# Eight of ten row norms: spread over the partitions through DRAM in place of products with the identity

## The chip, the cores and the metric

The kernel runs on one core of one Trainium2 chip. The metric is the time of one execution on the device in microseconds (us); three executions of the kernel before are shown, and their median is the time before. A profile is one execution taken by the hardware profiler. The engines are named as in the profile: PE is TensorE, DVE is VectorE, ACT is ScalarE, POOL is GpSimd and SP is SyncE, which here issues transfers.

## The reference, cut to what matters

Two blocks run one after the other over x of 512 tokens and 1024 features, in float32. The first has two hybrid layers (retention, pooling, neighbourhood attention and attention to a memory, side by side behind gates), each with a feed-forward part; the second has an "even" layer (sliding window and latent attention) and an "odd" one (dilated attention), each followed by cross attention to a memory and a feed-forward part.

```python
def rms_norm(x, g):
    xf = x.astype(jnp.float32)
    y = xf * lax.rsqrt(jnp.mean(xf * xf, axis=-1, keepdims=True) + EPS)
    return (y * g.astype(jnp.float32)).astype(x.dtype)
...
def hybrid_layer(x, mem, norm_mix_g, ...):
    h = rms_norm(x, norm_mix_g)
    proj = h @ w_in
...
    x = x + merged @ w_out
    a, g = jnp.split(rms_norm(x, norm_ffn_g) @ w_ffn_in, 2, axis=-1)
    return x + (jax.nn.silu(a) * g) @ w_ffn_out
...
    for layer in range(DEPTH):
        x = x + mixers[layer](rms_norm_2(x, mix_norms[layer]))
        x = x + memory_cross_attention(rms_norm_2(x, xn), rms_norm_2(mem, mn), wq, wkv, wo)
        x = x + swiglu(rms_norm_2(x, fn), wg, wu, wd)
    return rms_norm_2(x, final_norm)
```

So x is normalised ten times before a product (two hybrid layers, even, odd, two cross attentions, four feed-forward parts), and once at the end. Inside even, two more norms stand over the latent vectors cq and ckv.

## The kernel before, in words

x lies feature-major: eight tiles X of 128 features by 512 tokens. Next to it lies H, x times the gain, split into a high and a low part in float32r. A weight matrix is streamed in chunks of 512 KB: a transfer on SP's queue brings it into `ws` (two buffers), ACT casts it to the high part `wh` (L265, three buffers), DVE takes the difference `wl` (L266), and every product is three matmuls, high by high, low by high and high by low (L273 to L275, or L317 to L319 in the hybrid, even and odd layers where columns are 256 wide). A chunk feeds 24 matmuls. The results go to PSUM banks with the names p_acc, p_S and p_O; p_T is the bank of transposes and of the norms.

The product does not wait for the norm of x: it is made of x times the gain, and each result is multiplied afterwards, as it leaves PSUM, by 1/rms of its token. While x is updated, `prep` adds its squares into `acc`. `stats` then makes the norm: four small matmuls with a column of ones give the sum of each token, tokens on the partitions (a 128x4 tile); a Newton iteration on DVE (L340 to L347) makes `rtok_x` of it. To multiply a feature-major result, 1/rms must stand in a row over all tokens, the same on all 128 partitions: the tile `R_x`, 128x512. `spread` makes it: four fp32 matmuls of rtok, one column at a time broadcast to 128x128, with the identity (L368), into one p_T bank, and a copy by ACT (L371):

```python
        for i in range(4):
            nc.tensor.matmul(out=pb[:, 128 * i:128 * i + 128], lhsT=r[:, i:i + 1].to_broadcast([128, 128]),
                             rhs=self.ident, start=True, stop=True)
        R = self.tabp.tile([128, 512], F32, name="R_" + name, tag="R", bufs=3)
        nc.scalar.copy(R, pb)
```

Where R_x is used first: in a feed-forward part (`ffn`), DVE multiplies the first result of the gate by it (`fa`, L700). In the hybrid, even and odd layers it is multiplied into the rope tables (`ropeC`, L730, or `rope`), and `rope` (L480 to L491) empties the PSUM bank: four copies by ACT to `ru` (L484, L485), DVE's `ru` (L486) and `rc` (L488), which is the last to read the bank, and the sum (L491). In even, `norm_stats` is called twice more, for cq and ckv (`rtok_cq`, `rtok_ckv`, `R_cq`, `R_ckv`), a few instructions at a time beside sliding-window attention: scores (L476, L477) in p_S, DVE's and ACT's softmax into P (L519), transposes (L554) and their copy PT, and products with the values into p_O. The transposes of the memory (L664) and its products (`mh`, `ml`) follow there. The first hybrid layer weaves the neighbourhood attention in the same way between weight products (scores L476/L477, softmax L501 to L511, transposes L554, PT L561, values L928).

The order of the instructions on each engine is set by the scheduler of the language, which plays the program through a timeline of its own and puts weights 200 places ahead (AHEAD); the code's order is only its input. All transfers go by SP's queue. Among them the two that matter for comparison: `rpd<-rpb_p` writes 120 pieces of 192 bytes to DRAM (L1408), and `x<-xd` reads 256 KB.

Of the kernel before, what the change touches and what calls it, by code (L numbers as in the profile page):

```python
# [9 lines left out]
F32 = mybir.dt.float32  # L10
# [7 lines left out]
D = 1024  # L18
# [70 lines left out]
def run(gen):  # L89
    for _ in gen:  # L90
        pass


def weave(main, fill, rate, lead=0.0):

    due = lead
    for _ in main:
        due += rate
        while due >= 1.0:
            due -= 1.0  # L100
            next(fill, None)
# [29 lines left out]
def pipeline(pairs):  # L131

    prev = None
    for p, pair in enumerate(pairs):
        if p == 0 and pair.prep:
            pair.prep()
            yield
        for i in range(pair.n):
            state = pair.first(i)
            yield  # L140
            if prev:
                prev[0].second(*prev[1:])
                if prev[1] == prev[0].n - 1:
                    prev[0].done()
                yield
            prev = (pair, i, state)
            if i == 2 and p + 1 < len(pairs) and pairs[p + 1].prep:
                pairs[p + 1].prep()
    prev[0].second(*prev[1:])
    prev[0].done()  # L150
    yield


class Net:
# [196 lines left out]
                g.tensor_tensor(out=y, in0=y, in1=t, op=OP.mult)  # L351
        return y

    def norm_stats(self, acc, dim, name, want_bc=True):

        nc = self.nc
        ps = self.psum("T")
        for i in range(4):
            nc.tensor.matmul(out=ps[:, i:i + 1], lhsT=acc[:, 128 * i:128 * i + 128], rhs=self.ones, start=True, stop=True)
        r = self.rsqrt(ps[:, 0:4], 4, 1.0 / dim, self.sm.tile([128, 4], F32, name="rtok_" + name, tag="rtok", bufs=4), fast=True)  # L360
        return r, self.spread(r, name) if want_bc is True else None

    def spread(self, r, name):

        nc = self.nc
        pb = self.psum("T")
        for i in range(4):
            nc.tensor.matmul(out=pb[:, 128 * i:128 * i + 128], lhsT=r[:, i:i + 1].to_broadcast([128, 128]),  # L368
                             rhs=self.ident, start=True, stop=True)
        R = self.tabp.tile([128, 512], F32, name="R_" + name, tag="R", bufs=3)  # L370
        nc.scalar.copy(R, pb)  # L371
        return R

    def prep(self, k, g, start=False):
# [13 lines left out]
            gf = self.vec("final_norm_2", 8)  # L388
            nc.vector.tensor_scalar(out=self.X[k], in0=self.X[k], scalar1=gf[:, k:k + 1], scalar2=None, op0=OP.mult)

    def stats(self, want_bc=True):
        return self.norm_stats(self.acc, D, "x", want_bc)

    def head_stats(self, sq, nt, r):

# [957 lines left out]
    def cross(self, l, kv, g_next):  # L1353
        nc, a = self.nc, self.a
        p = f"l{l}_"
        mk, mv = kv()
        _, R = self.stats()
        heads = [None] * 4
        q = [self.at(name="xq") for _ in range(4)]

        def pair(h):
            st = {}
            c, b = h // 2, h % 2

            def first(i):
                if i == 0:
                    st["O"] = self.psum("O")
                Ps = []
                for t in range(2 * i, 2 * i + 2):
                    Sp = self.psum("S")[:, :256]  # L1370
                    nc.tensor.matmul(out=Sp, lhsT=q[h][:, 128 * t:128 * t + 128], rhs=mk[c][:, b, :], start=True, stop=True)
                    Ps.append(self.softmax(Sp, 256, X_SCALE))
                return Ps

            def second(i, Ps):
                pt = self.transposes([Ps[t][:, 128 * j:128 * j + 128] for j in range(2) for t in range(2)])
                for j in range(2):
                    nc.tensor.matmul(out=st["O"][:, 256 * i:256 * i + 256], lhsT=mv[c][:, j, 128 * b:128 * b + 128],
                                     rhs=pt[:, 256 * j:256 * j + 256], start=j == 0, stop=j == 1)

            def done():
                heads[h] = self.split(st["O"])
            return Pair(first, second, done, n=2)

        def project(c, tags):
            return self.proj_steps(self.H, a[p + "w_xq_2"], 256 * c, 256,
                                   lambda j, ps: nc.vector.tensor_tensor(out=q[2 * c + j], in0=ps, in1=R, op=OP.mult), tags=tags)

        Wo = a[p + "w_xo_2"]
        run(project(0, WIDE))  # L1390
        fill = project(1, ("acc",))
        weave(pipeline([pair(0), pair(1)]), fill, 0.5)
        run(fill)
        fill = self.residual_steps(heads[:2], Wo, 0, 2, 1.0, False, ("acc",), 0, 4)
        weave(pipeline([pair(2), pair(3)]), fill, 0.5)
        run(fill)
        self.residual(heads[2:], Wo, 2, 2, 1.0, g_next, WIDE, 0, 4)
        self.residual(heads, Wo, 0, 4, 1.0, g_next, WIDE, 4, 8)
# [121 lines left out]
```

## Time and profile before

| | |
|---|---|
| median of 3 executions | 3081.18 us (3078.11 to 3083.54) |
| profiled execution, its own time | 3081.58 us |
| its span in the profile | 3079.8 us |
| PE busy | 3011.1 us (98%) |
| DVE busy | 1706.3 us (55%) |
| ACT busy | 1248.5 us (41%) |
| POOL busy | 312.4 us (10%) |
| packets of the transfers | 288594, 285.61 MB, mean 93 GB/s |

The span runs from the first to the last instruction in the profile; the execution's own time holds a little more. Busy time is a share of the whole span. Matmuls overlap their neighbours, so the time that one holds the path is read from the chain or from the distance of two starts, not from its duration.

### The profile page before, as it was taken

The page shows a single profiled execution, that of the slowest core. Times are in us where ns is not written, and L with a number is a line of the kernel's source. Part 1 is how long each engine was busy: PE and PEld are TensorE (multiplying, and loading weights), DVE is VectorE, ACT ScalarE, POOL GpSimd, SP SyncE. Part 2 cuts the span into 40 slices and gives each one's busy share as a digit, 9 for nine tenths or more (in the row PEclk, how much of TensorE's full clock was granted, in tenths as well). Part 3 has the DMA queues.
Part 4 walks back from the last instruction along what each step waited for, and adds up shares of the span by engine and source line. Part 5 has one row for each costly group of instructions (what it writes and reads, how often), then busy time and mean ns, then how long its engine had stood idle before and what let it go on. Part 6 is the DMA issues. An engine that isn't in the chain of part 4 may idle for free.

```text
span 3079.8 us, 39014 instructions
## 1 busy us (share of the span) xinstructions
PE 3011.1 (98%) x15087; PEld 2479.5 (81%) x15087; DVE 1706.3 (55%) x2984; ACT 1248.5 (41%) x2102; POOL 312.4 (10%) x491
## 2 busy tenths in 40 slices
PE   7999999999999999999999899999999999999998
PEld 6777888888888878888888777788888777888887
DVE  7466465444565755654446676654446766464444
ACT  5445233222453533432224654432225766442222
POOL 4210120010132012010010000010010000010100
PEclk9999999999999999999999999999999999999999
DMA  5322243333332223333323222233333211233332
GB/s 170 104 64 71 92 127 96 96 97 99 126 116 87 82 83 109 119 95 98 96 89 96 78 61 62 72 96 96 96 89 96 69 56 62 89 103 96 96 96 82
DMA packets 288594, 285.61 MB, mean 93 GB/s; under 512 B 23700, under 2 KB 280089, under 8 KB 288409
## 3 DMA queue, kind: packets, MB, share of 16 engines
q1 hardware_dynamic: 288409, 283.13, 30.3%
q8 instruction: 118, 1.93, 0.3%
q14 instruction: 67, 0.55, 0.1%
HBM read 275.37 MB, written 7.71 MB: 92 GB/s over the span
## 4 chain that ended last, share of the span: by engine, by line
PE 90%; DVE 5%; DMA 1%; issue 1%; ACT 1%; POOL 1%; SPq 0%; DVEq 0%; ACTq 0%; POOLq 0%
PE p_acc L273 11%; PE p_acc L274 11%; PE p_acc L275 11%; PE p_S L273 7%; PE p_S L274 7%; PE p_S L275 7%; PE p_O L274 7%; PE p_O L275 7%; PE p_O L273 7%; PE p_acc L317 2%; PE p_acc L318 2%; PE p_acc L319 2%; PE p_T L554 2%; PE p_O L858 1%; DVE wl L266 1%
## 5 line engine op out<-in xcount | busy, mean ns | idle before, releaser
L266 DVE TENSOR_TENSOR wl<-ws,wh 128x1024 fp32r<-128x1024 f32 (+1 forms) x516 | 618.8, 1200 | 738.6 <-ACT wh L265 737.4
L265 ACT CAST wh<-ws 128x1024 fp32r<-128x1024 f32 (+1 forms) x516 | 516.7, 1002 | 1095.7 <-issue 352.9
L273 PE MATMUL p_acc<-hh,wh 128*128 128x512 f32 x1064 | 418.7, 394 | 4.4 <-DVE rs_t L344 1.7
L274 PE MATMUL p_acc<-hh,wl 128*128 128x512 f32 x1064 | 416.6, 392 | 0.0
L275 PE MATMUL p_acc<-hl,wh 128*128 128x512 f32 x1064 | 415.0, 391 | 0.0
L704 POOL TENSOR_TENSOR fa<-fa,R_x 128x512 f32<-128x512 f32 x88 | 115.2, 1310 | 1524.9 <-DVE fa L703 1524.9
L274 PE MATMUL p_O<-hh,wl 128*128 128x512 f32 x656 | 255.5, 390 | 0.0
L275 PE MATMUL p_O<-hl,wh 128*128 128x512 f32 x656 | 255.5, 389 | 0.0
L273 PE MATMUL p_O<-hh,wh 128*128 128x512 f32 x656 | 254.7, 389 | 0.0
L274 PE MATMUL p_S<-hh,wl 128*128 128x512 f32 x640 | 249.6, 391 | 2.7 <-DVE wl L266 2.7
L273 PE MATMUL p_S<-hh,wh 128*128 128x512 f32 x640 | 249.6, 392 | 2.4 <-ACT wh L265 2.4
L275 PE MATMUL p_S<-hl,wh 128*128 128x512 f32 x640 | 249.6, 391 | 0.0
L273 PEld LDWEIGHTS p_acc<-hh,wh 128*128 128x128 f32 x1064 | 199.7, 188 | 49.3 <-issue 3.6
L275 PEld LDWEIGHTS p_acc<-hl,wh 128*128 128x128 f32 x1064 | 199.7, 188 | 41.6 <-issue 0.8
L274 PEld LDWEIGHTS p_acc<-hh,wl 128*128 128x128 f32 x1064 | 199.9, 188 | 40.3 <-issue 1.7
L273 PE MATMUL p_acc<-ah,wh 128*128 128x512 f32 x468 | 185.0, 397 | 1.4 <-ACT ah L243 1.4
L274 PE MATMUL p_acc<-ah,wl 128*128 128x512 f32 x468 | 182.5, 390 | 0.0
L275 PE MATMUL p_acc<-al,wh 128*128 128x512 f32 x468 | 182.4, 393 | 0.0
L274 PEld LDWEIGHTS p_S<-hh,wl 128*128 128x128 f32 x640 | 120.8, 189 | 28.4 <-DVE wl L266 3.4
L274 PEld LDWEIGHTS p_O<-hh,wl 128*128 128x128 f32 x656 | 123.1, 188 | 25.5
L273 PEld LDWEIGHTS p_O<-hh,wh 128*128 128x128 f32 x656 | 123.1, 188 | 25.5
L275 PEld LDWEIGHTS p_O<-hl,wh 128*128 128x128 f32 x656 | 123.2, 188 | 25.3
(385 smaller groups left out, 5623.7 us busy)
## 6 DMA issues: line engine op xcount, KB each, us to landing
ws<-w_ffn_in SPq DMA_DIRECT2D x88, 512.0 KB, 3.6
ws<-w_gate SPq DMA_DIRECT2D x64, 512.0 KB, 3.7
ws<-l_w_gate SPq DMA_DIRECT2D x44, 512.0 KB, 4.0
ws<-l_w_up SPq DMA_DIRECT2D x44, 512.0 KB, 3.7
ws<-w_ffn_out SPq DMA_DIRECT2D x40, 512.0 KB, 3.5
ws<-l_w_down SPq DMA_DIRECT2D x40, 512.0 KB, 3.5
ws<-w_in SPq DMA_DIRECT2D x36, 512.0 KB, 3.8
ws<-l_w_qkv SPq DMA_DIRECT2D x24, 512.0 KB, 3.5
```

The costliest lines, as they stand in the source:

```text
L265: nc.scalar.copy(wh, st)
L266: nc.vector.tensor_tensor(out=wl, in0=st, in1=wh.bitcast(F32), op=OP.subtract)
L273: nc.tensor.matmul(out=out, lhsT=wh[part, k, cols], rhs=hh[part, hn], start=start, stop=False)
L274: nc.tensor.matmul(out=out, lhsT=wl[part, k, cols], rhs=hh[part, hn], start=False, stop=False)
L275: nc.tensor.matmul(out=out, lhsT=wh[part, k, cols], rhs=hl[part, hn], start=False, stop=stop)
L317: nc.tensor.matmul(out=o, lhsT=hh[:, t0:t0 + 128], rhs=wh[:, kk, :], start=k == 0, stop=False)
L318: nc.tensor.matmul(out=o, lhsT=hh[:, t0:t0 + 128], rhs=wl[:, kk, :], start=False, stop=False)
L319: nc.tensor.matmul(out=o, lhsT=hl[:, t0:t0 + 128], rhs=wh[:, kk, :], start=False, stop=k == K - 1)
L554: nc.tensor.transpose(pt[:, 128 * i:128 * i + 128], b, self.ident)
L704: nc.gpsimd.tensor_tensor(out=a, in0=a, in1=R, op=OP.mult)
L858: nc.tensor.matmul(out=O[64 * b:64 * b + 64, :], lhsT=rv[i // 2][:, i % 2, 64 * h:64 * h + 64], rhs=Ps[b], start=i == 0, stop=i == 3)
```

## The change

For eight of the ten norms of x, `stats` now calls `spread_far` in place of `spread`: a first transfer writes the 128x4 tile of rtok to a row of 512 numbers in DRAM (element by element, since token i*128+p lies on partition p), and a second reads that row into all 128 partitions of R. Both are issued on ACT's queue; the second waits there for the first to land. The two cross attentions (`near=True`) and cq and ckv keep `spread`. Each of the eight has a row of its own in DRAM.

```diff
--- before.py
+++ after.py
@@ -351,14 +351,14 @@
                 g.tensor_tensor(out=y, in0=y, in1=t, op=OP.mult)
         return y
 
-    def norm_stats(self, acc, dim, name, want_bc=True):
+    def norm_stats(self, acc, dim, name, want_bc=True, near=True):
 
         nc = self.nc
         ps = self.psum("T")
         for i in range(4):
             nc.tensor.matmul(out=ps[:, i:i + 1], lhsT=acc[:, 128 * i:128 * i + 128], rhs=self.ones, start=True, stop=True)
         r = self.rsqrt(ps[:, 0:4], 4, 1.0 / dim, self.sm.tile([128, 4], F32, name="rtok_" + name, tag="rtok", bufs=4), fast=True)
-        return r, self.spread(r, name) if want_bc is True else None
+        return r, (self.spread if near else self.spread_far)(r, name) if want_bc is True else None
 
     def spread(self, r, name):
 
@@ -369,6 +369,16 @@
                              rhs=self.ident, start=True, stop=True)
         R = self.tabp.tile([128, 512], F32, name="R_" + name, tag="R", bufs=3)
         nc.scalar.copy(R, pb)
+        return R
+
+    def spread_far(self, r, name):
+
+        nc = self.nc
+        self.spreads = getattr(self, "spreads", 0) + 1
+        row = self.dr.tile([1, 512], F32, name=f"row{self.spreads}", tag=f"row{self.spreads}")
+        R = self.tabp.tile([128, 512], F32, name="R_" + name, tag="R", bufs=3)
+        nc.scalar.dma_start(out=row.rearrange("o (i p) -> p (o i)", p=128), in_=r)
+        nc.scalar.dma_start(out=R, in_=row.to_broadcast([128, 512]))
         return R
 
     def prep(self, k, g, start=False):
@@ -388,8 +398,8 @@
             gf = self.vec("final_norm_2", 8)
             nc.vector.tensor_scalar(out=self.X[k], in0=self.X[k], scalar1=gf[:, k:k + 1], scalar2=None, op0=OP.mult)
 
-    def stats(self, want_bc=True):
-        return self.norm_stats(self.acc, D, "x", want_bc)
+    def stats(self, want_bc=True, near=False):
+        return self.norm_stats(self.acc, D, "x", want_bc, near)
 
     def head_stats(self, sq, nt, r):
 
@@ -1354,7 +1364,7 @@
         nc, a = self.nc, self.a
         p = f"l{l}_"
         mk, mv = kv()
-        _, R = self.stats()
+        _, R = self.stats(near=True)
         heads = [None] * 4
         q = [self.at(name="xq") for _ in range(4)]
 
```

In the new file the lines behind L373 stand ten lower (L554 is L564 there, L476 is L486). What the scheduler makes of it is shown at three places.

ACT in the first feed-forward part, around the copy of R_x (ft is the tanh of the gate, ah the high part of the hidden vector). Before:

```order
286 L246 ACTIVATE hh_109<-x_94,gain_566 128x512
287 L385 ACTIVATE sq<-x_94 128x512
288 L265 CAST wh<-ws 128x1024 x2
289 L371 COPY R_x<-p_T 128x512
290 L265 CAST wh<-ws 128x1024
291 L702 ACTIVATE ft<-fa 128x512 x2
292 L243 CAST ah<-fa 128x512
```

After:

```order
289 L246 ACTIVATE hh_109<-x_94,gain_563 128x512
290 L395 ACTIVATE sq<-x_94 128x512
291 L265 CAST wh<-ws 128x1024 x2
292 L380 DMA row_4589<-rtok_x 128x4x1
293 L381 DMA R_x<-row_4589 128x512
294 L712 ACTIVATE ft<-fa 128x512 x2
295 L265 CAST wh<-ws 128x1024
296 L243 CAST ah<-fa 128x512
```

The copy is gone and the two transfers stand in its place; the cast that followed the copy now follows the first two ft.

DVE in the even layer, in the sliding-window attention (ISA is the softmax, stack a copy of the queries for the scores, al a low part of the result, krot and kru the rope of the key, ml the memory's low part). Before:

```order
1417 L519 ISA P,sm_ms<-p_S,c_swa,nsink 128x256
1418 L519 ISA sm_ms 128x1
1419 L445 TENSOR_TENSOR stack<-swq_13817,stack 64x512
1420 L244 TENSOR_TENSOR al<-otR,ah 128x512
1421 L1181 TENSOR_TENSOR krot<-krot,kru 32x512
1422 L347 SCALAR_TENSOR_TENSOR rtok_ckv<-rs_t,rtok_ckv 128x4
1423 L1102 TENSOR_TENSOR rope<-cos_11280,R_cq 128x512
1424 L1103 TENSOR_TENSOR rope<-sin_11281,R_cq 128x512
1425 L344 TENSOR_TENSOR rs_t<-rtok_ckv 128x4
1426 L346 SCALAR_TENSOR_TENSOR rs_t<-rs_t,rs_a 128x4
1427 L347 SCALAR_TENSOR_TENSOR rtok_ckv<-rs_t,rtok_ckv 128x4
1428 L247 SCALAR_TENSOR_TENSOR ml<-p_T,gain_11254,mh 128x256 x7
```

After, the stretch in which the last step of rtok_ckv stands now:

```order
1402 L247 SCALAR_TENSOR_TENSOR hl_96<-cq_13888,gain_11245,hh_95 128x512
1403 L247 SCALAR_TENSOR_TENSOR hl_98<-cq_13889,gain_11245,hh_97 128x512
1404 L347 SCALAR_TENSOR_TENSOR rtok_ckv<-rs_t,rtok_ckv 128x4
1405 L247 SCALAR_TENSOR_TENSOR hl_100<-cq_13890,gain_11245,hh_99 128x512
1406 L247 SCALAR_TENSOR_TENSOR hl_102<-cq_13891,gain_11245,hh_101 128x512
1407 L501 TENSOR_TENSOR swq_13802<-rc,ru 128x512
1408 L529 ISA P,sm_ms<-p_S,c_swa,nsink 128x256
1409 L529 ISA sm_ms 128x1
1410 L266 TENSOR_TENSOR wl<-ws,wh 128x1024
1411 L247 SCALAR_TENSOR_TENSOR hl_104<-cq_13892,gain_11245,hh_103 128x512
1412 L1189 TENSOR_TENSOR kru<-p_acc,rope 32x512
1413 L1190 TENSOR_TENSOR krot<-p_acc,rope 32x512
```

Before, the last step of rtok_ckv (the third L347 of it) stood right ahead of ml, behind the stacks, al, krot and the rope products of R_cq. After, it stands ahead of hl of the last cq tiles, kru and krot; the stacks, the rest of krot and the rope products follow further on.

PE in the first hybrid layer's neighbourhood attention. Before:

```order
1074 L273 MATMUL p_acc<-hh_109,wh 128x512
1075 L274 MATMUL p_acc<-hh_109,wl 128x512
1076 L476 MATMUL p_S<-stack 128x256
1077 L275 MATMUL p_acc<-hl_110,wh 128x512
1078 L476 MATMUL p_S<-stack 128x256
1079 L928 MATMUL p_O<-PT,nvt 64x128 x4
1080 L554 MATMUL p_T<-small_cst,P 128x128 x3
1081 L477 MATMUL p_S<-stack 128x256
1082 L554 MATMUL p_T<-small_cst,P 128x128
1083 L477 MATMUL p_S<-stack 128x256
1084 L273 MATMUL p_acc<-ah,wh 128x512
1085 L274 MATMUL p_acc<-ah,wl 128x512
```

After:

```order
1069 L273 MATMUL p_acc<-hh_109,wh 128x512
1070 L274 MATMUL p_acc<-hh_109,wl 128x512
1071 L275 MATMUL p_acc<-hl_110,wh 128x512
1072 L564 MATMUL p_T<-small_cst,P 128x128 x4
1073 L486 MATMUL p_S<-stack 128x256 x2
1074 L487 MATMUL p_S<-stack 128x256 x2
1075 L564 MATMUL p_T<-small_cst,P 128x128 x4
1076 L938 MATMUL p_O<-PT,nvt 64x128 x8
1077 L273 MATMUL p_acc<-ah,wh 128x512
1078 L274 MATMUL p_acc<-ah,wl 128x512
1079 L275 MATMUL p_acc<-al,wh 128x512
1080 L273 MATMUL p_acc<-ah,wh 128x512
```

Before, scores, values and transposes stood in smaller groups (four value products, then three and one transposes, with scores between). After, four transposes, four scores, four transposes and eight value products stand in one block, and the weight products follow behind it. On PE the rows of L368 for x are gone at all eight places.

## Rows read from the trace of the kernel before

**Rows 1.** The page, chain that ended last, by engine.

```profile
PE 90%; DVE 5%; DMA 1%; issue 1%; ACT 1%; POOL 1%; SPq 0%; DVEq 0%; ACTq 0%; POOLq 0%
```

**Rows 2.** L368 by its forms: duration min/median/max ns, first and last start.

```profile
L368 PE MATMUL p_T<-small_cst,rtok_x x80: 270/275/275, 39.9 to 2730.3; 128*128 128x128 f32 x80
```

**Rows 3.** The chain from 501 to 504: start, us, what.

```profile
502.18 0.89 PE p_T L368 x8
503.07 0.23 PE p_acc L275
```

**Rows 4.** The timeline, second hybrid layer: start, us, engine, line [idle before <-releaser].

```profile
880.51 0.16 DVE L347 SCALAR_TENSOR_TENSOR rtok_x<-rs_t,rtok_x 128x4 f32<-128x4 f32 x1
...
886.29 0.59 ACT L371 COPY R_x<-p_T 128x512 f32<-128x512 f32 x1 [1.88 <-PE p_T L368]
...
898.40 0.68 DVE L488 TENSOR_TENSOR rc<-p_acc,ropeC 128x512 f32<-128x512 f32 x1
...
900.72 0.28 PE L317 MATMUL p_acc<-wh,hh 128*128 128x256 f32 x1
```

**Rows 5.** The timeline, odd layer.

```profile
2353.94 0.16 DVE L347 SCALAR_TENSOR_TENSOR rtok_x<-rs_t,rtok_x 128x4 f32<-128x4 f32 x1
...
2359.61 0.59 ACT L371 COPY R_x<-p_T 128x512 f32<-128x512 f32 x1 [1.42 <-PE p_T L368]
...
2367.20 0.68 DVE L488 TENSOR_TENSOR rc<-p_O,rope 128x512 f32<-128x512 f32 x1
...
2371.09 0.28 PE L317 MATMUL p_O<-wh,hh 128*128 128x256 f32 x1
```

**Rows 6.** The timeline, even layer.

```profile
1661.66 0.16 DVE L347 SCALAR_TENSOR_TENSOR rtok_x<-rs_t,rtok_x 128x4 f32<-128x4 f32 x1
...
1667.33 0.59 ACT L371 COPY R_x<-p_T 128x512 f32<-128x512 f32 x1 [1.42 <-PE p_T L368]
...
1681.61 0.68 DVE L488 TENSOR_TENSOR rc<-p_acc,rope 128x512 f32<-128x512 f32 x1
...
1685.11 0.39 PE L273 MATMUL p_acc<-hh,wh 128*128 128x512 f32 x1
```

**Rows 7.** The timeline, ffn after the second hybrid layer.

```profile
1310.19 0.09 DVE L347 SCALAR_TENSOR_TENSOR rtok_x<-rs_t,rtok_x 128x4 f32<-128x4 f32 x1
...
1315.64 1.29 DVE L700 TENSOR_TENSOR fa<-p_S,R_x 128x512 f32<-128x512 f32 x2 [3.82 <-ACT R_x L371]
...
1320.98 0.39 PE L273 MATMUL p_S<-hh,wh 128*128 128x512 f32 x1
```

**Rows 8.** DMA issues: KB each, us to landing; and the queue of all.

```profile
q1 hardware_dynamic: 288409, 283.13, 30.3%
...
mem<-mem SPq DMA_DIRECT2D x16, 256.0 KB, 5.0
x<-xd SPq DMA_DIRECT2D x16, 256.0 KB, 3.1
nvt<-nvd SPq DMA_DIRECT2D x64, 32.0 KB, 1.8
rpd<-rpb_p SPq DMA_DIRECT2D x16, 22.5 KB, 3.3
```

**Rows 9.** The timeline, ACT in the first ffn.

```profile
504.04 1.05 ACT L265 CAST wh<-ws 128x1024 fp32r<-128x1024 f32 x1 [0.34 <-PE p_acc L275]
```

**Rows 10.** The timeline, even attention.

```profile
1740.50 0.16 DVE L347 SCALAR_TENSOR_TENSOR rtok_ckv<-rs_t,rtok_ckv 128x4 f32<-128x4 f32 x1
...
1740.81 0.77 PE L368 MATMUL p_T<-small_cst,rtok_ckv 128*128 128x128 f32 x2 [3.73 <-DVE rtok_ckv L347]
```

**Rows 11.** One window: us, busy us of each engine (x count), PEclk, DMA, GB/s.

```profile
1728.00:1744.00 16.00, 7.95 (x32) 6.38 (x33) 12.23 (x29) 6.28 (x15) 1.11 (x1) 0.60 0.21 66
```

**Rows 12.** The timeline, first hybrid layer's neighbourhood attention.

```profile
234.45 0.33 PE L554 MATMUL p_T<-small_cst,P 128*128 128x128 f32 x1
...
235.26 0.59 ACT L561 COPY PT<-p_T 128x512 f32<-128x512 f32 x1 [0.37 <-PE p_T L554]
```

## The prediction

> **What bounds the kernel now.** I read the page first: the chain that ended last runs over TensorE for 90% of the span, over DVE for 5% and over DMA for 1% [rows 1]. So a change pays by TensorE time taken off the queue or by a gap closed, and costs by a gap opened. The profiled execution took 3081.58 us for a span of 3079.8 (1.8 around it); the median of the runs is 3081.18, 0.4 less.
>
> Next I asked for the line that spreads a norm. L368 appears for x eighty times, which is ten norms of eight passes (four fp32 products of two passes each), one pass 275 ns [rows 2]. Passes overlap, so the cost on the path is read from the chain: eight passes stand there with 0.89 us in one piece, between ordinary products of 0.23 us [rows 3]. The other seven places that change stand there with the same, within 0.02.
>
> Then I read, place by place, how late R comes and who waits for it: from the end of rtok's last step to the end of ACT's copy, and from the first product that is multiplied by R (it empties a PSUM bank) to the TensorE instruction that wants that bank [rows 4 to 7].
>
> **The change part by part.** *Removed: eight times 0.89 us of TensorE work.* All eight lie on the chain, with TensorE full on both sides, so 8 x 0.89 = 7.1 us go. ACT also loses eight copies of 0.59 us [rows 4], which buys nothing, because ACT is on the chain for 1% [rows 1].
>
> *Added: two transfers in a row on ACT's queue, per place.* The first writes 2 KB in 512 pieces of 4 bytes; the second waits for its landing and reads 2 KB into each of 128 partitions, 256 KB together. The trace has no such pair. For the write the nearest rows are 1.8 us for nvt (32 KB) and 3.3 us for rpd (22.5 KB in 192-byte pieces) [rows 8]. q1's 288409 packets took 30.3% of 16 engines' 3079.8 us, 51.8 ns each [rows 8]; 512 pieces over 16 engines are 32 x 0.052 = 1.7 us, an estimate for the pieces alone. I take 3.4, near rpd, because the pieces are smaller than any here. For the read the nearest is x<-xd, 256 KB in 3.1 us; mem<-mem, 256 KB in 5.0, is the upper bound [rows 8]. Issue and the two waits I put at 0.2, so R is late by L = 3.4 + 3.1 + 0.2 = 6.7 us after rtok, with bounds 1.8 + 3.1 = 4.9 and 3.3 + 5.0 = 8.3, somewhat more if 4-byte pieces are dearer than rpd's. Before, the same stretch took 6.2 us in the first example, since TensorE reached the spread late and ACT the copy behind it. So R comes at about the same time as now.
>
> The Trainium skill, "DMA: Bandwidth & Descriptors", section "Anatomy of one DMA", gives a fixed 2.0 us and bytes over 436 GB/s per transfer (for GpSimd's path); by it the pair would take an estimated 2.0 + 2.6 = 4.6 us and R would come earlier than now, and the sum below would lose its 0.1. The trace's 256 KB read takes 3.1 rather than 2.6.
>
> *What a late R costs.* In the second hybrid layer rtok ends at 880.51 + 0.16 = 880.67 and R at 886.88 (6.2 us). DVE works without a pause from there to `rc<-p_acc`, which frees its bank at 899.08; TensorE wants a p_acc bank at 900.72 [rows 4]. That is 1.64 of room, less 0.9 because TensorE now comes earlier: it stalls when L passes 6.2 + 0.7 = 6.9. In odd: R 6.1 after rtok, bank free at 2367.88, wanted 2371.09, so 6.1 + 3.2 - 0.9 = 8.4 [rows 5]. In even: 6.1 + 2.8 - 0.9 = 8.0 [rows 6]. In the ffn after the second hybrid layer: R after 5.4 (DVE takes it up at 1315.64, rtok ended at 1310.28), first bank free 0.65 later (half of the 1.29), wanted at 1320.98, so 5.4 + 4.7 - 0.9 = 9.2 [rows 7]. The four others have more room than that. So the stall is the sum of what L exceeds 6.9, 8.0, 8.4 and 9.2: nothing at 6.7, 1.1 at 8, 7.5 at 10, 15.5 at 12. At 6.7, so close to the first bound, I book 0.1.
>
> *ACT's queue.* The second transfer waits at ACT's head for the first to land, some 3.4 us, and the weight casts and rope copies stand behind it (the order of ACT above, for the first ffn). The cast that followed the copy in the first ffn ran at 504.04 [rows 9]; a chunk feeds 24 products of 0.23 us [rows 3], 5.4 us, and there are three buffers of cast chunks, so TensorE has more than one chunk, over 5.4 us, to go on with and 3.4 are covered. If that cover were gone, each place would cost up to 3.4. SP's and POOL's queues get nothing new.
>
> *Moved: even's attention.* Here the scheduler's order changes more than the removed rows. Before, the last step of rtok_ckv stands on DVE behind four stacks, al, krot and two rope products; it ends at 1740.66, and TensorE sat idle 3.73 us for it before its L368 [rows 10]; DVE was without a pause before it. In the order of after, that step stands ahead of kru, and both near spreads run early, so the products of the memory, which need nothing from there, no longer queue behind rtok_ckv. What is late next is PT, which the PV products ahead of L664 need. Bounds: nothing, if PT takes over the whole wait, and 3.73 if it goes. I take 2, the middle. The stretch holds more: in 1728 to 1744 TensorE worked 7.95 of 16 us, at a granted clock of 0.60 [rows 11], that is, much of it at the 1.2 GHz level after sitting idle for DVE. If it never sat idle there, 8 us and part of the doubled matmul times would come back.
>
> *Moved: the neighbourhood attention of the first hybrid layer.* Before, products with weights stand between the scores and the next transposes. After, at the place shown, two sets of scores, two of four transposes and eight PV products follow each other without a filler. The PV products wait for ACT's copy of the transposes. Before, that copy ended 1.40 us after the first of such transposes began (235.85 against 234.45), and TensorE went on meanwhile [rows 12]; the four transposes themselves are some 0.5 of that, so with nothing to go on with, such a place costs 0.9 us. Elsewhere in this layer, and in odd's attention, products change places in both directions, and I can't tell from the order which way the whole moves: 0, with +-3.5 (four such places).
>
> **The sum.** 3081.58 - 7.1 + 0.1 - 2 + 0 = 3072.6; less 0.4 to the median, 3072.
>
> **The rivals.** *R late, the saving eaten.* L of 8 to 10, if the read takes mem's 5.0 or the small write more than rpd: 1.1 to 7.5 us of stall at four places. Against the 7.1 saved and without even's gain that gives 3075 to 3082. For it: a pair of dependent transfers, and the first bound only 0.2 away. Against it: three of the four bounds are 8 or more.
>
> *The weave turns out worse.* The lost fillers cost 3.5 to 7 us with nothing won: 3081.2 - 7.1 + 3.5 = 3077.6, up to 3081. For it: the place shown. Against it: the hybrid layers' TensorE gaps are few now.
>
> *Slower: the pieces of 4 bytes.* One mechanism: the row's write. If a piece takes 200 ns in its engine and not 52, 32 of them take 4.75 us more, L is 11.45, and four places stall 13.3 us in all; that is 7.1 + 6.2 (even's 2 not counted), from where the change is slower by more than 0.2%. At 280 ns L is 14, the four stall some 23.5 us, the other four begin to, and the time is about 3081 - 7 + 25 = 3099. For it: the smallest pieces in the rows are rpd's 192 bytes. Against it: these land in 3.3 us, hardly more than x<-xd's 3.1 with eleven times the bytes [rows 8]. The Trainium skill, same page, "Rules for kernel authors", says that a strided last dimension lowers to one descriptor per element and that transfers under 64 KB are mostly overhead, and "Specifications" that below 512 B the engine reads, modifies and writes; all three hold for this write, and would push towards this case. No row here shows a price for it.
>
> *More is won.* Even's half-clock stretch shrinks: the bound 3.73 plus half of the other gaps and of the slow matmuls, 6 to 12 us more than the spreads: 3081.2 - 7.1 - 6 = 3068 and down to 3062. Against it: DVE is busy 12.23 of those 16 us [rows 11], and its work stays.
>
> **Chances.** The forecast (3067 to 3075) 0.58; R late 0.14; a worse weave 0.10; slower 0.10; more won, below 3067, 0.08. A measurement of this kernel tells 0.2%, 6.2 us, from no change: below 3075.0 is faster, above 3087.3 slower. The first and last case are faster, 0.66; the second and third the same, 0.24; 0.10 slower. The range takes in the forecast, R late and the weave, and half of the last: 3064 to 3082.
>
> **What would show it.** Right: L368 left with 16 passes for x (two norms of cross attention) and the 16 for cq and ckv; R's transfer landing 6 to 7 us after rtok's end; p_acc of the second hybrid layer near the room computed; fewer us before L664 in even. Wrong: TensorE idle with DVE, and behind it R's transfer, as releaser at rc (hybrid, even, odd) or fa; the row's write above 5 us; wh casts that end TensorE waits behind ACT's DMA wait; new idle at PV or the transposes of the first hybrid layer.

## The result and the profile after

The changed kernel takes 3125.95 us (median of 5, 3124.01 to 3128.58) against 3080.99 beside it: a ratio of 1.015, 95% interval 1.0136 to 1.0164. That is 45 us slower, where 9 us faster was forecast, and outside the range. Of the cases of the prediction it is the fourth, the write of 4-byte pieces, and more of it than was worked out there, though not by the price per piece that the case named (below).

The page of the changed kernel: span, busy time, the new queue of ACT, and the chain that ended last by engine and by line.

```profile
span 3123.3 us, 38893 instructions
...
PE 3016.4 (97%) x15023; PEld 2481.9 (79%) x15023; DVE 1706.2 (55%) x2984; ACT 1243.3 (40%) x2094; POOL 314.7 (10%) x491
...
q10 hardware_dynamic: 5376, 2.11, 0.4%
...
PE 83%; DVE 7%; DMA 5%; ACT 2%; issue 2%; SPq 1%; POOL 0%; DVEq 0%; ACTq 0%; POOLq 0%
PE p_acc L273 10%; PE p_acc L274 10%; PE p_acc L275 10%; PE p_S L274 7%; PE p_S L273 7%; PE p_S L275 7%; PE p_O L274 7%; PE p_O L275 7%; PE p_O L273 7%; DMA row<-rtok_x 3%; PE p_acc L317 2%; PE p_acc L318 2%; PE p_acc L319 2%; DVE wl L266 2%; PE p_T L564 2%
```

TensorE's share of the chain fell from the 90% of [rows 1] to 83%, DMA's rose from 1% to 5%, and one line of it, the write of the row, is 3% by itself. The sum can be made from these lines and the table of before. TensorE sat idle 3079.8 - 3011.1 = 68.7 us before and 3123.3 - 3016.4 = 106.9 now: 38.2 more. It was also busy 5.3 us longer, although 7.1 us of spreads are gone: 12.4 us of the same matmuls, at a lower granted clock (mean 0.988, before 0.991). 38.2 + 12.4 - 7.1 = 43.5, the difference of the spans. The 12.4 is rough: against p16 and spaced below, whose TensorE work is the same, TensorE is busy 13.1 and 7.9 us longer.

The spreads are gone as meant. L368 by its forms, to compare with [rows 2]:

```profile
L368 PE MATMUL p_T<-small_cst,rtok_x x16: 270/275/275, 1961.5 to 2672.9; 128*128 128x128 f32 x16
```

Next, the chain through the first feed-forward part, with the products of TensorE left out (start, us, what).

```profile
505.81 11.20 DMA row<-rtok_x
...
517.03 4.13 DMA R_x<-row
...
521.19 0.70 DVE fa L710
...
521.91 0.64 ACT ft L712
...
523.11 1.04 ACT wh L265
...
524.17 1.98 DVE wl L266
```

The write stands in the chain with 11.20 us, the read behind it with 4.13. Then the tanh `ft` runs, and only behind that the weight cast, which TensorE waits for: ACT's queue is in order, and its head needed R. In [rows 9] that cast ran at 504.04. rtok had ended at 505.19 here, so R came 16.0 us after it, against 6.6 before.

The timeline in the second hybrid layer, to compare with [rows 4] (columns as there):

```profile
893.50 0.16 DVE L347 SCALAR_TENSOR_TENSOR rtok_x<-rs_t,rtok_x 128x4 f32<-128x4 f32 x1
...
893.69 0.38 ACTq L380 DMA_DIRECT2D row<-rtok_x  x1
...
903.27 0.33 ACTq L381 DMA_DIRECT2D R_x<-row  x1
...
907.53 0.69 DVE L740 TENSOR_TENSOR ropeC<-ropeC,R_x 128x512 f32<-128x512 f32 x1 [1.50 <-DMA R_x<-row]
...
909.34 0.68 DVE L498 TENSOR_TENSOR rc<-p_S,ropeC 128x512 f32<-128x512 f32 x1
...
910.17 0.36 PE L317 MATMUL p_S<-wh,hh 128*128 128x256 f32 x1 [2.98 <-DVE rc L498]
```

893.69 to 903.27 is the write, 9.6 us; the read lands at 907.51; R is 13.9 us after rtok, and the bank that `rc` frees ends TensorE's idle time. Over the eight places the write took 8.8 to 11.6 us (from its issue to that of the read behind it), and R came 13.2 to 18.4 us after rtok.

The two longest waits, in the first hybrid layer and in the feed-forward part after the second:

```profile
52.68 0.69 DVE L740 TENSOR_TENSOR ropeC<-ropeC,R_x 128x512 f32<-128x512 f32 x1 [8.14 <-DMA R_x<-row]
...
59.24 0.80 PE L274 MATMUL p_acc<-hh,wl 128*128 128x512 f32 x1 [6.39 <-DVE wl L266]
```

```profile
1347.20 0.77 PE L273 MATMUL p_S<-hh,wh 128*128 128x512 f32 x1 [6.47 <-DVE fa L710]
```

In the first, DVE stands 8.14 us at `ropeC` for R. The weight part `wl`, which needs nothing of R, stands behind it on DVE, and TensorE waits for `wl` and not for a bank. In the second, TensorE waits for the bank that `fa` frees.

What a stall leaves behind, and the even attention: windows with us, busy us of PE, PEld, DVE, ACT and POOL, PEclk, DMA share and GB/s.

```profile
1345.00:1350.00 5.00, 2.80 (x7) 2.25 (x8) 1.98 (x3) 2.86 (x4) 0.09 (x1) 0.58 0.03 10
1350.00:1355.00 5.00, 5.00 (x18) 3.99 (x17) 4.89 (x6) 1.98 (x4) 2.50 (x2) 0.74 0.31 94
1761.00:1777.00 16.00, 8.41 (x59) 6.38 (x56) 15.60 (x29) 10.50 (x26) 1.03 (x1) 0.96 0.21 67
```

After the 6.47 us without work that end at 1347.20, TensorE is granted 0.58 and 0.74 in the next two windows, partly the 1.2 GHz level, while it is busy all of the second. The third row is even's attention, at the place of [rows 11] 33 us later: the clock is 0.96 where it was 0.60, and TensorE works 8.41 us where it worked 7.95.

### The profile page after: what moved, and what is told of

Read it like the earlier page. It is cut to its first block, busy times and chain, and to the rows that moved or that the text cites. A ratio compares the mean times of both kernels' runs of the same rounds, so it can differ in the third digit from the quotient of the medians.

```text
span 3123.3 us, 38893 instructions
## 1 busy us (share of the span) xinstructions
PE 3016.4 (97%) x15023; PEld 2481.9 (79%) x15023; DVE 1706.2 (55%) x2984; ACT 1243.3 (40%) x2094; POOL 314.7 (10%) x491
## 4 chain that ended last, share of the span: by engine, by line
PE 83%; DVE 7%; DMA 5%; ACT 2%; issue 2%; SPq 1%; POOL 0%; DVEq 0%; ACTq 0%; POOLq 0%
PE p_acc L273 10%; PE p_acc L274 10%; PE p_acc L275 10%; PE p_S L274 7%; PE p_S L273 7%; PE p_S L275 7%; PE p_O L274 7%; PE p_O L275 7%; PE p_O L273 7%; DMA row<-rtok_x 3%; PE p_acc L317 2%; PE p_acc L318 2%; PE p_acc L319 2%; DVE wl L266 2%; PE p_T L564 2%
## 5 line engine op out<-in xcount | busy, mean ns | idle before, releaser
L273 PEld LDWEIGHTS p_S<-hh,wh 128*128 128x128 f32 x640 | 121.7, 190 | 39.2 <-issue 8.4
```

The lines of the kernel that those rows point to most:

```text
L273: nc.tensor.matmul(out=out, lhsT=wh[part, k, cols], rhs=hh[part, hn], start=start, stop=False)
```

## The experiments

Theory A is that the write of 4-byte pieces is slow by itself, and that everything else follows from R's lateness. Rival B is that it is slow because of where it runs, on ACT's queue beside the weights. A second question is what costs: the late R, or ACT standing behind the write. A program's stages are compared by the end of the sixteenth `fa` product on POOL in each feed-forward part, which gives four stages with two of the changed places each. The shift of each stage against before, in us:

| kernel | first hybrid, ffn | second hybrid, ffn | even, cross, ffn | odd, cross, ffn | time of the runs, ratio to before |
|---|---|---|---|---|---|
| changed | +13.0 | +15.9 | +7.7 | +7.5 | 3125.95, 1.015 |
| p16 | +0.4 | +0.2 | -5.2 | -3.5 | 3074.65, 0.9987 (0.9978 to 0.9997) |
| spaced | -0.1 | +1.0 | -6.2 | +1.0 | 3073.68, 0.9984 (0.9974 to 0.9993) |
| twice | +0.7 | +6.2 | -1.9 | -0.2 | 3085.25, 1.0019 (1.0010 to 1.0028) |
| thrice | +6.9 | +15.8 | +3.2 | +6.6 | 3111.66, 1.0111 (1.0097 to 1.0125) |
| split | +12.3 | +16.3 | +6.6 | +8.1 | 3125.02, 1.015 (1.0136 to 1.0164) |
| idle | +5.4 | +4.0 | -0.7 | +3.1 | 3093.04, 1.0047 (1.0032 to 1.0062) |
| even16 | -1.8 | +0.2 | -5.7 | +0.8 | 3075.12, 0.9991 (0.9982 to 1.0000) |

The shifts are of one profiled execution each. Two of the runs, probe and probe2, have the program of before unchanged up to its end, and show what a repeat is worth: -2.4 and -1.1 us in the first stage, +0.1 and +0.1 in the second, +1.5 and -0.1 in the third, +2.4 and 0.0 in the fourth. The ratio and its 95% interval are of all runs; it need not be the quotient of the two medians. Times of before in these sessions: 3078.62 (p16, idle, turned), 3078.55 (fixed, split, twice), 3078.66 (ffn4, spaced, thrice, even16).

TensorE's idle time around each of the eight changed places, in us, in the 38 us from 3 before the end of rtok to 35 behind it:

| kernel | first hybrid | ffn | second hybrid | ffn | even | ffn | odd | ffn |
|---|---|---|---|---|---|---|---|---|
| before | 0.2 | 0.0 | 0.4 | 0.0 | 0.0 | 0.0 | 0.0 | 0.0 |
| changed | 9.5 | 3.7 | 6.3 | 6.5 | 6.7 | 2.9 | 3.5 | 1.1 |
| p16 | 3.3 | 0.0 | 1.4 | 0.0 | 0.0 | 0.0 | 0.0 | 0.0 |
| twice | 4.6 | 0.0 | 3.3 | 0.8 | 2.6 | 0.0 | 2.9 | 0.0 |
| thrice | 7.8 | 0.0 | 5.2 | 5.2 | 6.2 | 0.8 | 4.4 | 1.0 |
| split | 9.2 | 2.6 | 6.6 | 5.8 | 7.3 | 1.8 | 5.7 | 2.0 |
| idle | 5.5 | 0.0 | 3.4 | 0.0 | 0.0 | 0.0 | 3.2 | 0.0 |

In the two repeats of before the first place has 0.7 and 1.9, and the others are as here. Of the changed kernel's 40 us, about 23 end with a weight part, `wh` or `wl`, and about 17 with a product that R is multiplied into (`rc`, `fa`, and `swvT` in even).

**probe: the transfers by themselves.** Behind the kernel's end, on SP's queue, each waiting for the one before:

```diff
+            nc.sync.dma_start(out=row.rearrange("o (i p) -> p (o i)", p=128), in_=src)
+            nc.sync.dma_start(out=Rp, in_=row.to_broadcast([128, 512]))
...
+            nc.sync.dma_start(out=wide.rearrange("o (i p c) -> p (o i) c", p=128, c=16)[:, :, 0:1], in_=src.unsqueeze(2))
```

Expected: 

> The kernel before, with a row of transfers behind its end, each waiting for the one before: writes of 512 pieces of 4 bytes, 128 of 4, 128 of 16, 4 of 512, and 512 of 4 spaced 64 bytes apart in DRAM, each followed by the 256 KB read of one row into all partitions. Theory A (the pieces set the write's time): about 10 us for 512 pieces, as in the changed kernel, some 4 us for the two of 128 pieces, 2 to 3 us for 4 pieces, and 10 for the spaced ones. Rival B (the write is slow for where it runs, beside weights and on ACT's queue): all writes within 2 to 4 us here. The read about 4 us in both.

The issues on SP's queue, second round. A write's time is the distance from its issue to that of the read behind it (L1457: 512 pieces of 4 bytes; L1459: 128 of 4; L1461: 128 of 16; L1463: 4 of 512; L1465: 512 of 4, 64 bytes apart).

```profile
3114.58 0.37 SPq L1457 DMA_DIRECT2D pwide<-x  x1
3123.32 0.32 SPq L1458 DMA_DIRECT2D R_probe<-pwide  x1
3128.15 0.32 SPq L1459 DMA_DIRECT2D pwide<-x  x1
3136.19 0.32 SPq L1460 DMA_DIRECT2D R_probe<-pwide  x1
3140.45 0.32 SPq L1461 DMA_DIRECT2D pwide<-x  x1
3141.86 0.32 SPq L1462 DMA_DIRECT2D R_probe<-pwide  x1
3145.78 0.26 SPq L1463 DMA_DIRECT2D pwide<-x  x1
3146.94 0.32 SPq L1464 DMA_DIRECT2D R_probe<-pwide  x1
3150.10 0.37 SPq L1465 DMA_DIRECT2D pwide<-x  x1
3152.43 0.32 SPq L1466 DMA_DIRECT2D R_probe<-pwide  x1
```

512 pieces take 8.7 us, 128 pieces 8.0, and 512 pieces that stand 64 bytes apart 2.3. Over three rounds: 8.4 to 10.5, 6.6 to 8.0, and 1.9 to 2.3. 128 pieces of 16 bytes take 1.4, 4 of 512 bytes 1.2. So the write is slow with nothing beside it and on another queue: rival B falls. But theory A as written falls too, since the number of pieces matters little; what matters is whether the small pieces lie side by side.

**probe2: how near is too near.**

```diff
+            for gap in (1, 2, 4, 8, 16):
+                d = wide[:, 0:128 * gap].rearrange("o (p c) -> p (o c)", c=gap)[:, 0:1]
+                nc.sync.dma_start(out=d, in_=src[:, 0:1])
```

Expected: 

> The kernel before with another row of transfers behind its end: 128 pieces of 4 bytes, 4, 8, 16, 32 and 64 bytes apart in DRAM, then 128 pieces of 8, 16 and 32 bytes side by side. If what costs is that neighbouring pieces share a stretch of DRAM: 7 us at 4 apart, less at 8 and 16, under 2 from 64 on (and the step tells how long the stretch is); 8-byte pieces between the 7 us of 4 bytes and the 1.4 us of 16. If only the number of pieces counts, all the same.

128 pieces of 4 bytes, 4, 8 and 16 bytes apart, and 128 of 8 bytes side by side (L1464), second round:

```profile
3121.35 0.32 SPq L1460 DMA_DIRECT2D pwide<-x  x1
3128.19 0.32 SPq L1461 DMA_DIRECT2D R_probe<-pwide  x1
3133.18 0.32 SPq L1460 DMA_DIRECT2D pwide<-x  x1
3136.11 0.32 SPq L1461 DMA_DIRECT2D R_probe<-pwide  x1
3140.19 0.32 SPq L1460 DMA_DIRECT2D pwide<-x  x1
3141.59 0.32 SPq L1461 DMA_DIRECT2D R_probe<-pwide  x1
...
3154.71 0.32 SPq L1464 DMA_DIRECT2D pwide<-x  x1
3157.68 0.32 SPq L1465 DMA_DIRECT2D R_probe<-pwide  x1
```

6.8 us at 4 apart, 2.9 at 8 (6.1 in the first round, beside the kernel's last stores), 1.4 at 16, and 1.4 at 32 and 64. Pieces of 8 bytes take 2.9 and 3.0, of 16 bytes 1.4 and 2.0. The step is at 16 bytes: pieces that start less than 16 bytes apart delay each other. That they share 16 bytes of DRAM is a reading that fits; no run tells it from the distance alone.

**p16: 16-byte pieces in the kernel.** The only edit. The order on TensorE, POOL and SP is that of the changed kernel; on ACT and DVE a few instructions of one feed-forward part, after the second hybrid layer, change places.

```diff
-        nc.scalar.dma_start(out=row.rearrange("o (i p) -> p (o i)", p=128), in_=r)
+        nc.scalar.dma_start(out=row.rearrange("o (p i) -> p (o i)", p=128), in_=r)
```

Expected: 

> The changed kernel, with the row laid out so that each partition writes its four numbers as one piece of 16 bytes: 128 pieces in place of 512 (the columns of R then stand in another order, so the result is another one). The order of instructions is the same on every engine. Theory A (pieces): the write takes 4 to 5 us, R comes 8 to 9 us after rtok, and the time is 3078 to 3090. Rival B (queue and neighbours, not pieces): the write keeps 9 to 11 us and the time 3126.

The chain in the second hybrid layer:

```profile
881.12 3.35 DMA row<-rtok_x
884.49 3.89 DMA R_x<-row
```

The write takes 3.35 us there (1.4 to 3.8 over the eight places) and R comes 5.8 to 7.3 us after rtok, but 11.5 in the first hybrid layer. The time is 3074.65, 51 us below the changed kernel and 4 below before; write and time are lower than either theory had them. One line of layout was the whole loss. It does not bring the whole gain: TensorE idles 3.3 and 1.4 us at the two hybrid layers (table; before, 0.2 to 1.9 in three executions, and 0.4).

**spaced: the same 512 pieces, 16 bytes apart.**

```diff
-        row = self.dr.tile([1, 512], F32, name=f"row{self.spreads}", tag=f"row{self.spreads}")
+        row = self.apart[:, 0:512]
...
+        nc.scalar.dma_start(out=self.apart.rearrange("o (i p c) -> p (o i) c", p=128, c=4)[:, :, 0:1], in_=r.unsqueeze(2))
```

Expected: 

> The changed kernel with its 512 pieces of 4 bytes written 16 bytes apart in DRAM; the read takes the first 2 KB of that stretch (three quarters of R are zeros, so the result is another one). If the loss comes from pieces that share 16 bytes: the write takes 2 to 4 us, the time is near the run with 16-byte pieces, 3072 to 3080. If it comes from the number of pieces or their 4 bytes as such: write 9 to 11 us, 3120 to 3130.

The timeline in the second hybrid layer (`apart` is the row):

```profile
880.61 0.38 ACTq L384 DMA_DIRECT2D apart<-rtok_x  x1
...
885.13 0.33 ACTq L385 DMA_DIRECT2D R_x<-apart  x1
...
888.27 0.69 DVE L744 TENSOR_TENSOR ropeC<-ropeC,R_x 128x512 f32<-128x512 f32 x1 [0.38 <-DMA R_x<-apart]
```

The write takes 4.5 us here (2.2 to 4.8 over the places), R comes 7.7 us after rtok, and the time is 3073.68. With pieces of 4 bytes and as many of them, the loss is gone: it was neither the size of the pieces nor their number, but neighbours less than 16 bytes away.

**twice and thrice: lateness without the slow write.** p16 with the read of R issued two and three times in a row. ACT stands behind these reads, too, and the scheduler moves other work with them (TensorE's order in twice differs from p16's at 1246 of 15023 places).

```diff
+        nc.scalar.dma_start(out=R, in_=row.to_broadcast([128, 512])); nc.scalar.dma_start(out=R, in_=row.to_broadcast([128, 512]))
```

Expected of the first: 

> The run with 16-byte pieces (columns of R in another order, so the result is another one) with the read of R issued twice, the second behind the first: R comes some 4 us later, 10 to 11 us after rtok. By the prediction's reading of the room (6.9, 8.0, 8.4, 9.2 us at four places) the stalls are 7.5 to 11.5 us, so 3082 to 3087 where the single read gave 3074.65. If each stall also brings back TensorE at half clock, 3088 to 3095. If lateness of 10 us is still covered, 3075 to 3079.

Expected of the second: 

> As the run that reads R twice, with a third read: R some 13 to 14 us after rtok, without any 4-byte write (columns in another order, so the result is another one). If lateness alone makes the changed kernel's loss, it lies between the twice-read run (10 us late, 3085) and the changed kernel (13 to 18 us late, 3126): 3104 to 3118. If the 4-byte write costs by something else too, such as holding up the weights: 3086 to 3100.

R comes 9.2 to 10.3 us after rtok in the first (16.1 in the first hybrid layer), and 13.0 to 15.3 in the second (21.0). One TensorE row of each: even in the first, the feed-forward part after the second hybrid layer in the second.

```profile
1691.01 0.47 PE L273 MATMUL p_acc<-hh,wh 128*128 128x512 f32 x1 [2.58 <-DVE rc L498]
```

```profile
1340.93 0.77 PE L273 MATMUL p_S<-hh,wh 128*128 128x512 f32 x1 [5.15 <-DVE fa L710]
```

10 us of lateness give 10.6 us over p16, where the prediction's four bounds give 7.5 to 11.5; 13 to 15 us give 37. In the second stage the thrice-read kernel loses 15.8 us, the changed one 15.9, with the same lateness (14.2 to 15.3 and 13.9 to 15.6). So a late R makes that stage's loss without a slow write. ACT is held up in both kernels; the next run tells the two apart. In twice, the idle time at the four places with a bound is 2.9, 0.8, 2.6 and 2.9 us more than before, where the bounds give 3.3, 0.7, 2.3 and 1.8 at its lateness.

**split: ACT set free.** The read on POOL's queue.

```diff
-        nc.scalar.dma_start(out=R, in_=row.to_broadcast([128, 512]))
+        nc.gpsimd.dma_start(out=R, in_=row.to_broadcast([128, 512]))
```

Expected: 

> The changed kernel with the second transfer on POOL's queue, so that ACT no longer stands behind the 4-byte write; the write itself and the lateness of R stay (14 to 16 us after rtok). If late R is most of the loss: 3110 to 3126. If ACT's blocked queue is most of it: 3085 to 3105. The run with the idle pair, 14 us over before, speaks for the first.

The timeline in the second hybrid layer:

```profile
904.22 0.61 POOL L381 DMA_DIRECT2D R_x<-row  x1 [26.42 <-DMA row<-rtok_x]
...
908.37 0.69 DVE L740 TENSOR_TENSOR ropeC<-ropeC,R_x 128x512 f32<-128x512 f32 x1 [10.36 <-DMA R_x<-row]
...
911.00 0.55 PE L317 MATMUL p_S<-wh,hh 128*128 128x256 f32 x1 [4.51 <-DVE rc L498]
```

POOL waits for the write in ACT's place, so ACT no longer stands behind the transfers. R is as late (15.4 us after rtok), TensorE waits 4.51 us for the same `rc`, and the time stays at 3125.02. ACT's queue, ACTq, holds the writes alone here, which gives their price in the engines (packets, MB, share of 16 engines):

```profile
q10 hardware_dynamic: 4224, 0.02, 0.1%
```

That is about 12 ns a packet (0.1% of 16 times 3123.1 us, and 0.1 is a rounded figure). The write is slow, but not by the time that its pieces are counted with in the engines.

**idle: ACT blocked, R on time.** The spread on TensorE, and the pair issued besides, into a tile that nobody reads.

```diff
+        R = self.spread(r, name)
+        if not near:
+            self.spread_far(r, name)
```

Expected: 

> The kernel before, which spreads on TensorE, with the same two transfers issued on ACT's queue as well at the eight places, into a tile that nobody reads. R is not late here, but ACT still stands 10 us behind the write. If the late R is what costs (theory A1): 3081 to 3086. If ACT's blocked queue costs by itself, its casts and copies late (rival A2): 3100 to 3125.

TensorE in the first hybrid and in the odd layer:

```profile
58.15 0.79 PE L274 MATMUL p_acc<-hh,wl 128*128 128x512 f32 x1 [4.47 <-DVE wl L266]
```

```profile
2383.07 0.35 PE L317 MATMUL p_O<-wh,hh 128*128 128x256 f32 x1 [3.16 <-DVE rc L503]
```

3093.04, 14 us over before, between the two expectations: the idle pair costs by itself, with the order on TensorE, DVE and ACT that of before. The likeliest cause is ACT's block; the pair's own 256 KB read, and the one of three R buffers that it takes, are in the figure too. TensorE loses it in the first hybrid, the second hybrid and the odd layer (table); the feed-forward parts and even cover a write of 9 to 12 us. ACT's block adds nothing on top of a late R, as split shows. Why is argued only: the casts stand behind work that waits for R in any case, as `ft` does in the first feed-forward part.

**even16: even's norm alone.** p16's layout for even, all others near.

```diff
+        rt, R = self.stats(near=False)
```

Expected: 

> Only the even layer's norm goes through DRAM, in 16-byte pieces (columns of R in another order, so the result is another one); all others spread on TensorE. On DVE and TensorE the order of even's attention is then as in the changed kernel. If the moved rtok_ckv is worth what the prediction's bounds say beside the 0.9 of the one spread: 3072 to 3077. If the moved attention gains nothing: 3077 to 3080.

Even's attention, at the place of [rows 11] less 1.7 us (columns as there):

```profile
1726.00:1742.00 16.00, 9.77 (x63) 8.84 (x64) 12.57 (x26) 7.56 (x20) 1.03 (x1) 0.89 0.19 63
```

TensorE works 9.77 of 16 us at 0.89, where it was 7.95 at 0.60, and the third stage is 5.7 us shorter; only 0.9 of it is the spread. The other 4.8 (a repeat of before differs by up to 1.5) come from the new order, which the scheduler makes when even's R comes from a transfer: 3.0 us less idle time in the stage, the rest matmuls at a higher clock. The 3.73 us for rtok_ckv [rows 10] are gone. What ends last now is the copy R_cq and, behind it, the softmax:

```profile
1727.74 1.16 PE L368 MATMUL p_T<-small_cst,rtok_ckv 128*128 128x128 f32 x8 [2.38 <-ACT R_cq L371]
...
1735.51 0.39 PE L486 MATMUL p_S<-ah,stack 128*128 128x256 f32 x1 [3.81 <-DVE sm_ms L529]
```

The time is 3.5 us below before, at the edge of what can be told (interval up to 1.0000).

**turned, fixed and ffn4: three ways to a row in order.** The first turns rtok by a TensorE transpose and writes 4 pieces of 512 bytes; the second makes rtok for every fourth token with strided weights, so that 16-byte pieces stand in order; the third has ACT write the squares in that order, for the feed-forward parts alone.

```diff
+        nc.tensor.transpose(pt[:4, :128], r, self.ident)
+        nc.vector.tensor_copy(out=rr, in_=pt[:4, :128])
...
+            cols += [acc.rearrange("k (p i) -> k i p", i=4)[:, i, :] for i in range(4)]
...
+            nc.scalar.activation(out=sq.rearrange("k (i p) -> k p i", i=4), in_=self.X[k].rearrange("k (p i) -> k p i", i=4), func=AF.Square)
```

Expected of the first: 

> The changed kernel, with rtok first turned by one TensorE transpose into four rows of 128 and copied by DVE, so that the row is written in 4 pieces of 512 bytes. Theory A: the write takes 2 to 3 us, R comes 7 to 8 us after rtok, the time is 3072 to 3084. Rival B: write and time as in the changed kernel, 3120 to 3130.

Expected of the second: 

> The changed kernel with the right result and 16-byte pieces: four more small matmuls with ones take tokens in steps of four, so that token 4p+i lies on partition p and the row is written in order, 128 pieces of 16 bytes (the feed-forward parts need these four alone; hybrid, even and odd keep the old four too). Theory A (the 4-byte pieces side by side are the whole loss): write 1.4 to 4 us, R 6 to 8 us after rtok, time 0.998 to 1.000 of before. Rival (the gain of the run with 16-byte pieces came from its wrong columns or from luck of the order): 1.002 or more.

Expected of the third: 

> A version with the right result: only the four feed-forward norms go through DRAM, since they need R alone. The squares for them are written by ACT in the order 4p+i, at no extra instruction, so that the row is written in 128 pieces of 16 bytes; hybrid, even and odd spread on TensorE as before. Four times 0.89 us of TensorE go, R comes 6 to 7 us after rtok where the room is 9 and more: 3073 to 3077 against 3078.6 in these sessions (0.998 to 0.9995). If the strided squares on ACT or the pair cost something: 3079 to 3084.

turned took 3089.15 (1.0036, 1.0023 to 1.0049): a miss. The write takes 1.2 us in the first feed-forward part, but the transpose stands behind other products in TensorE's queue, and R comes 8.6 to 11.3 us after rtok (15.7 in the first hybrid layer). fixed took 3086.68 (1.0020, 1.0012 to 1.0029): a miss too, for another reason. The loads and matmuls with ones by their line:

```profile
L364 PEld LDWEIGHTS p_T<-small_cst,acc x136: 186/192/332, 27.6 to 3073.1; 128*128 128x128 f32 x136
L364 PE MATMUL p_T<-small_cst,acc x136: 164/250/393, 27.9 to 3073.1; 128*128 128x1 f32 x136
```

A load of strided weights takes up to 332 ns where others take 192; TensorE's busy time with the matmuls of this line grows from 12.5 us before to 23.5, more than the eight spreads gave. ffn4 took 3078.44 (0.9997, 0.9988 to 1.0006): no difference, and between its two expectations. Its result is another one, against what was meant; the cause was not looked for. None of the three is better than before, and a better one was not found.

## Why the prediction was wrong

**The step that failed** is the write of the row: "I take 3.4, near rpd, because the pieces are smaller than any here". It took 8.8 to 11.6. Neither of the two rows that were to bound it shows neighbours below 16 bytes: rpd's pieces have 192 bytes, and are no nearer to this case for being the smallest. The bound "somewhat more if 4-byte pieces are dearer" had no number, and the range rested on it. With the 1.4 to 4.8 us that p16 and spaced have, L was 5.8 to 8.7 at seven of the eight places, about the 6.7 of the forecast. Their times, 3074.65 and 3073.68, lie in the range, but they are 4.0 and 5.0 us below the before of their own sessions, half of the 9 that was forecast.

**The second step** is what a late R holds up. The prediction gave it one path, the bank that the first multiplied result frees, and for ACT's queue booked nothing: "over 5.4 us, to go on with and 3.4 are covered". In the trace instructions that wait for R also stand in front of the weight parts on ACT and DVE, whose work runs in order: about 23 of the 40 us around the eight places end with `wh` or `wl`. This is also where "the four others have more room than that" broke, which had no number: they lost 9.3, 3.7, 2.9 and 1.1 us, 17 together. The four places with a bound lost 5.9, 6.5, 6.7 and 3.5 us at 13.9, 15.6, 14.6 and 14.6 us of lateness (second hybrid, its feed-forward part, even, odd), where the bounds give 7.0, 6.4, 6.6 and 6.2. So three of the four were read about rightly, and odd's was not: its waits end with `wh` and `wl` there.

**The rival that came true** gave 3099 at 14 us. Besides the places without a number, a stall costs more than its idle time: the same matmuls took 8 to 13 us longer, at a lower mean clock, which the sum had no term for. And the rival came true in its outcome alone. Its mechanism was a price per piece, 200 to 280 ns in the engine; but 128 pieces took 6.6 to 8.0 us and 512 pieces 8.4 to 10.5, and the packets of the writes are counted with about 12 ns.

The rule of the Trainium skill, "DMA: Bandwidth & Descriptors", section "Specifications", that transfers below 512 bytes are read, modified and written, pointed to the right side. Its threshold is not what the runs show: 128 pieces of 16 bytes took 1.4 us, like 4-byte pieces 16 bytes apart, and hardly more than 4 pieces of 512 (1.2); only neighbours less than 16 bytes away were slow. The Trainium skill, same page, section "Rules for kernel authors", warns of one descriptor per element; 512 pieces, 64 bytes apart, took 1.9 to 2.3 us.

**What held.** The 0.89 us of a spread, as TensorE time: in the second stage, which the same program repeats within 0.1 us, TensorE is busy 797.3 us before and 796.4 in ffn4, with one spread less. That all eight lie on the chain held for seven: around the first one, at 39.9 us, the chain of [rows 1] runs over transfers and DVE. And in time the saving came only in part: in p16 and spaced the second stage has two spreads less and is no shorter (+0.2, +1.0), with R 7.3 and 7.7 us late at the hybrid layer, past its bound of 6.9. Most of what these two kernels gain comes in even's stage (-5.2 and -6.2), and even16, which changes even's norm alone, is 3.5 us faster by itself.

**What was too small:** even's moved attention, put at 2 us with a bound of 3.73 for rtok_ckv. In even16 it is 4.8; the clock gave back part, as the case "more is won" had it. PT was not what came next, but R_cq and the softmax. The weave of the first hybrid layer, 0 with 3.5 either way, can't be told from the 1 to 2 us by which the first stage varies; p16's +0.4 there holds an R that is 11.5 us late.

**What stays open** is why neighbours less than 16 bytes apart wait for one another, and where the time of such a write is spent.

## What to carry to other kernels

Before a small tile is written to DRAM across its partitions, look at how near neighbouring pieces lie: here they had to be 16 bytes long or 16 apart. Or try the transfer by itself behind a finished kernel, which costs one run. Put a number on the room of every place where a result is multiplied late, not only of the tightest, and look at what else stands behind the late instruction on its engine: here it was the weights. Count the clock too: after 6.47 us without work TensorE came back at 0.58 and 0.74. Work that is taken off the busiest engine is worth its time only if what replaces it, with all waits in a row, is not later than it was.

## What the runs showed of the hardware that was not expected

A write of 128 pieces of 4 bytes side by side took 6.6 to 8.0 us, one of 512 pieces 8.4 to 10.5; 16 or more bytes apart, 128 took 1.4, and 64 bytes apart 512 took 1.9 to 2.3. A load of weights that takes every fourth fp32 took up to 332 ns where a dense one took 192. The read of 2 KB into all partitions took 3.0 to 5.1 us in the quiet probe, its median 4.2, and so more than the 3.1 of a plain 256 KB read [rows 8].
